# A two-layer hybrid decoder step: column halves, one order for the whole program, weights loaded twice

## The chip, the cores and the metric

The kernel runs on all 8 NeuronCores of one Trainium2 chip. Each core computes one prompt sequence and 16 sample sequences with the whole network; the cores do not talk to each other. The metric is the device time of the slowest core, in us. An execution can fall into a slow state, in which the cores of one die show a lower granted clock; only fast executions are compared here. The granted clock is the share of full speed that the profile shows for TensorE. TensorE, VectorE, ScalarE and GpSimd are PE, DVE, ACT and POOL in the profile's lines; PEld is TensorE's weight load.

## The reference, cut to what matters

```python
# per layer, prompt (2064 tokens a core) and sample (16 x 8 tokens a core) share the weights
x = x + 0.5 * swiglu(rmsnorm(x, norm_ffn1[l]), w_ffn1_gu[l], w_ffn1_down[l])   # D 1024, D_FF 2816
x = x + mixer(rmsnorm(x, norm_mix[l]), ...)                                    # RG-LRU group + gated linear attention
x = x + 0.5 * swiglu(rmsnorm(x, norm_ffn2[l]), w_ffn2_gu[l], w_ffn2_down[l])
# after two layers: rmsnorm(x, norm_final)
```

Both mixer groups carry a state along the sequence (a scan; a 64 x 128 matrix per head), so the tiles of a mixer follow each other. FFN columns are independent of each other. That difference is what the change uses.

## The kernel before

The 2192 columns lie in five tiles; each FFN and each mixer takes all of them before the next begins, with barriers around the mixer.

```python
TILES = [(0, 400), (400, 512), (912, 512), (1424, 512), (1936, 256)]
# ...
            ffn(l, 0, base, do_norm=not prenormed)
            full_barrier()
            if do_mixer:
                mixer(l, base + NJ)
                full_barrier()
            # ... ffn(l, 1, ...)
```

The root mean square of a norm is a Sqrt on ScalarE and a reciprocal on VectorE; a mixer has 5 such tiles for its norm and 20 for the head norms:

```python
P.op("act", lambda h: h.activation(out=rsa[:, :n], in_=psN[:, :n], func=AF.Sqrt, scale=1.0 / D, bias=EPS), ...)
P.op("dve", lambda h: h.reciprocal(out=rsa[:, :n], in_=rsa[:, :n]), ...)
```

An FFN chunk is 128 of the 2816 FFN columns, and the ring is the set of buffers into which the weights are loaded in turn. One slot of the ring (11 slots) holds gate, up and down columns of one chunk, 768 KB; the mixer's weights are 10 slots, loaded once per layer. Inside an FFN step or a mixer a small list scheduler orders the instructions; across them it does not look.

## Time and profile before

| | before |
|---|---|
| median | 3657 us (3654 to 3697, 5 runs) |
| TensorE busy | 2850 us, 78% |
| VectorE / ScalarE busy | 1820 us, 50% / 971 us, 27% |
| mean granted clock | 0.88 |
| HBM read | 189 MB |

The busy share of TensorE is no good measure of how near it is to its peak: the Trainium skill says so ("Perfetto Trace Analysis", "Identifying the Most-Contended Engine"), and the trace agrees that the two differ: in the first 43 us of the changed kernel TensorE is busy 15.8 us with matmuls priced at 8.0.

### The profile page before, as it was taken

What the parts mean: (1) busy time and instruction counts of PE and PEld (TensorE: products, weight loads), DVE (VectorE), ACT (ScalarE), POOL (GpSimd) and SP (SyncE); (2) the same over time, 40 slices, a digit from 0 to 9 for tenths busy, and PEclk for the clock granted to TensorE, in tenths of its full rate; (3) what the DMA queues carried; (4) which work ended last, traced back from release to release, by engine and by line L of the source; (5) the groups of instructions that cost most, each with busy time, mean ns of one, the idle gap of its engine ahead of it and who ended that gap; (6) DMA issues with size and microseconds to landing.
All of it is one profiled execution on the core that took longest, in us unless ns stands there. A gap on an engine that the chain in (4) does not pass through costs nothing.

```text
span 3655.7 us, 43632 instructions; the slowest of 8 cores (3628.5 to 3655.7 us)
## 1 busy us (share of the span) xinstructions
PE 2850.2 (78%) x14312; PEld 1389.2 (38%) x14312; DVE 1820.4 (50%) x3210; ACT 971.4 (27%) x1762; POOL 75.3 (2%) x147
## 2 busy tenths in 40 slices
PE   1899998577664379999879999956756536999994
PEld 0455553232222235554435554422223212555542
DVE  2433344666674454334543334456676546443345
ACT  2211112544552231111221111154454323111122
POOL 2000000000000000000000000000000000000000
PEclk9999999788876589999989999977878757999997
DMA  9022223000002441111111111110000135111002
GB/s 200 1 35 35 35 45 54 1 1 1 1 1 35 46 68 35 35 35 35 27 27 35 35 35 35 36 29 1 1 1 1 13 44 93 33 37 27 1 19 81
DMA packets 70715, 119.74 MB, mean 33 GB/s; under 512 B 42560, under 2 KB 47328, under 8 KB 70496
## 3 DMA queue, kind: packets, MB, share of 16 engines
q0 software_dynamic: 18320, 85.52, 13.4%
q1 hardware_dynamic: 52176, 31.42, 4.3%
q8 instruction: 122, 2.00, 0.2%
q14 instruction: 97, 0.79, 0.1%
HBM read 188.72 MB, written 13.71 MB: 55 GB/s over the span
## 4 chain that ended last, share of the span: by engine, by line
PE 66%; DVE 12%; DMA 7%; ACT 7%; issue 5%; SPq 2%; DVEq 0%; ACTq 0%
PE ps L460 18%; PE ps L433 18%; PE ps L438 18%; PE ps L650 5%; PE ps L962 3%; DMA scr<-S 2%; SPq L368 2%; PE ps L762 2%; DVE scr L412 2%; DMA cTo<-scr 2%; PE ps L396 1%; DVE scr L934 1%; ACT L708 1%; DVE scr L409 1%; ACT scr L394 1%
## 5 line engine op out<-in xcount | busy, mean ns | idle before, releaser
L438 PE MATMUL ps<-scr,ring 128*128 128x512 bf16 (+2 forms) x3520 | 850.1, 349 | 12.5 <-DVE scr L446 12.5
L433 PE MATMUL ps<-scr,ring 128*128 128x512 bf16 (+2 forms) x3520 | 855.3, 350 | 1.6 <-ACT scr L444 1.4
L460 PE MATMUL ps<-scr,ring 128*128 128x512 bf16 (+2 forms) x3520 | 707.5, 357 | 108.0 <-DVE x L464 106.4
L446 DVE TENSOR_TENSOR scr<-ps,scr 128x512 bf16<-128x512 f32 (+2 forms) x440 | 252.5, 610 | 1050.0 <-PE ps L438 868.2
L444 ACT ACTIVATE scr<-ps 128x512 f32<-128x512 f32 (+2 forms) x440 | 214.9, 533 | 1585.6 <-PE ps L433 1390.4
L464 DVE SCALAR_TENSOR_TENSOR x<-ps,x 128x512 f32<-128x512 f32 (+2 forms) x960 | 563.8, 612 | 88.7 <-PE ps L460 74.7
L460 PEld LDWEIGHTS ps<-scr,ring 128*128 128x128 bf16 x3520 | 342.0, 100 | 453.4 <-issue 175.3
L438 PEld LDWEIGHTS ps<-scr,ring 128*128 128x128 bf16 x3520 | 345.0, 98 | 326.0 <-issue 20.5
L433 PEld LDWEIGHTS ps<-scr,ring 128*128 128x128 bf16 x3520 | 342.1, 98 | 317.4 <-issue 20.8
L650 PE MATMUL ps<-scr,ring 128*128 128x512 bf16 (+4 forms) x1360 | 398.9, 433 | 73.9 <-ACT scr L662 40.5
L650 PEld LDWEIGHTS ps<-scr,ring 128*128 128x128 bf16 (+1 forms) x1360 | 148.0, 115 | 235.8 <-issue 180.0
L962 PE MATMUL ps<-scr,ring 128*128 128x512 bf16 (+2 forms) x640 | 179.8, 404 | 59.4 <-DVE scr L748 25.1
L396 PE MATMUL ps<-scr,ones 128*128 128x512 bf16 (+2 forms) x240 | 101.9, 447 | 132.9 <-ACT scr L394 109.1
L394 ACT ACTIVATE scr<-x 128x512 bf16<-128x512 f32 (+2 forms) x240 | 127.1, 562 | 256.5 <-PE ps L396 103.8
L409 DVE RECIPROCAL scr<-scr 128x512 f32<-128x512 f32 (+2 forms) x30 | 86.7, 2890 | 144.0 <-ACT scr L407 144.0
L762 PE MATMUL ps<-ring,scr 128*128 128x256 bf16 (+1 forms) x576 | 113.2, 278 | 46.7 <-DVE scr L412 45.4
L412 DVE SCALAR_TENSOR_TENSOR scr<-x,cols_sb,scr 128x512 bf16<-128x512 f32 (+2 forms) x240 | 144.5, 669 | 4.1 <-DVE scr L409 1.0
L377 POOL DMA_DIRECT2D ring<-wslots x108 | 57.2, 536 | 3287.9 <-PE ps L433 1722.7
L962 PEld LDWEIGHTS ps<-scr,ring 128*128 128x128 bf16 x640 | 66.2, 109 | 141.5 <-issue 108.4
L934 DVE RECIPROCAL scr<-scr 128x512 f32<-128x512 f32 (+2 forms) x40 | 115.5, 2887 | 7.4 <-ACT scr L932 7.4
L966 DVE TENSOR_TENSOR x<-ps,x 128x512 f32<-128x512 f32 (+2 forms) x80 | 47.9, 613 | 125.8 <-PE ps L762 69.9
L396 PEld LDWEIGHTS ps<-scr,ones 128*128 128x128 bf16 x240 | 23.9, 102 | 198.4 <-issue 190.5
(140 smaller groups left out, 1712.4 us busy)
## 6 DMA issues: line engine op xcount, KB each, us to landing
ring<-wslots POOLq DMA_DIRECT2D x108, 768.0 KB, 14.8
scr<-S SPq DMA_DIRECT2D x16, 512.0 KB, 5.4
x<-xT SPq DMA_DIRECT2D x24, 256.0 KB, 16.9
yT<-scr SPq DMA_DIRECT2D x24, 256.0 KB, 2.0
Sos<-scr SPq DMA_DIRECT2D x8, 512.0 KB, 4.7
x<-xT SPq DMA_DIRECT2D x8, 200.0 KB, 23.3
yT<-scr SPq DMA_DIRECT2D x8, 200.0 KB, 1.9
x<-xT SPq DMA_DIRECT2D x8, 128.0 KB, 8.0
```

Source lines behind the costliest of these rows:

```text
L394: P.op("act", lambda h, kc=kc, sqa=sqa: h.activation(out=sqa[:, :n], in_=x[:, kc, s:s + n], func=AF.Square), reads=[("x", kc, ti)], writes ...
L396: P.op("pe", lambda h, kc=kc, sqa=sqa: h.matmul(psN[:, :n], lhsT=ones[:], rhs=sqa[:, :n], start=(kc == 0), stop=(kc == KC - 1)), reads=[sq ...
L412: P.op("dve", lambda h, kc=kc: h.scalar_tensor_tensor(out=dst_fn(kc, s, n), in0=x[:, kc, s:s + n], scalar=cols[:, gcol + kc:gcol + kc + 1] ...
L433: P.op("pe", lambda h, kc=kc, sl=sl, gb=gb: h.matmul(psG[gb][:, :n], lhsT=ring[:, sl, kc * 128:(kc + 1) * 128], rhs=xn[:, kc, s:s + n], st ...
L438: P.op("pe", lambda h, kc=kc, sl=sl, gb=gb: h.matmul(psU[gb][:, :n], lhsT=ring[:, sl, 1024 + kc * 128:1024 + (kc + 1) * 128], rhs=xn[:, kc ...
L444: P.op("act", lambda h, gb=gb, sb=sb: h.activation(out=sg[:, sb, :n], in_=psG[gb][:, :n], func=AF.Silu), reads=[("psG", gb)], writes=[("sg ...
L446: P.op("dve", lambda h, gb=gb, sb=sb, jj=jj: h.tensor_tensor(out=hbuf[:, hb, jj, :n], in0=psU[gb][:, :n], in1=sg[:, sb, :n], op=ALU.mult), ...
L460: P.op("pe", lambda h, mc=mc, sl=sl, db=db, jj=jj: h.matmul(psD[db][:, :n], lhsT=ring[:, sl, 2048 + mc * 128:2048 + (mc + 1) * 128], rhs=h ...
L464: P.op("dve", lambda h, mc=mc, db=db: h.scalar_tensor_tensor(out=x[:, mc, s:s + n], in0=psD[db][:, :n], scalar=0.5, in1=x[:, mc, s:s + n], ...
L650: P.op("pe", lambda h, kc=kc, lhs=lhs: h.matmul(mU[ub][:m, :n], lhsT=lhs, rhs=xnt[:, kc, :n], start=(kc == 0), stop=(kc == KC - 1)), reads ...
L762: P.op("pe", lambda h, kc=kc, pr=pr, rv=rv, cs=cs, cl=cl: h.matmul(mV[:cl, pr * 256:(pr + 1) * 256], lhsT=xnt[:, kc, cs:cs + cl], rhs=rv[: ...
L962: P.op("pe", lambda h, mc=mc, ic=ic, rsl=rsl, pos=pos, ub=ub: h.matmul(mU[ub][:, :n], lhsT=ring[:, rsl, pos * 1024 + mc * 128:pos * 1024 + ...
```

## The change

Its intent: never let TensorE stand, by running the mixer of one half of the columns under the FFN of the other. It is a rewrite of nearly all lines; this is its core, abridged, with some hunks in words. Of the instructions that are ready, the scheduler takes the lowest prio first.

```diff
-TILES = [(0, 400), (400, 512), (912, 512), (1424, 512), (1936, 256)]
+TILES = [(0, 272), (272, 384), (656, 384), (1040, 384), (1424, 384), (1808, 384)]
+HALVES = [[0, 1, 2], [3, 4, 5]]
-R = 11                         # slots of gate + up + down
+NGU, NDN, NPG = 6, 5, 7        # slots: gate/up, down, mixer page
...
+        for l in range(2):
+            ffn(l, 0, 0, first=(l == 0))
+            # ... norms of half 1
+            ffn(l, 0, 1)
+            mixer(l, 0)
+            # ... norms of half 0
+            ffn(l, 1, 0)
+            mixer(l, 1)
+            # ... norms of half 1
+            ffn(l, 1, 1, after=final_norm if l == 1 else None)
+        P.run(**cfg)           # one list scheduler over all instructions; PSUM banks are given out by it
...
-    Sqrt on ACT, reciprocal on DVE
+    P.op("act", [Ln(scale, bias=EPS), Exp(scale=-0.5)], ..., tbl="L")
...
+    pick on TensorE: mixer matmuls prio 0, FFN matmuls prio 1
```

FFN weights are loaded once per half and the mixer's 28 pages once per tile. Smaller things change too: Silu replaces a Tanh form in the head gate, the GeLU takes one VectorE pass fewer, 128-partition operations replace pairs of 64-partition ones, and the small recurrent states go in and out in single transfers.

## The prediction

> **What bounds the kernel now.** I read the slices first (part 2 of the page), to see where TensorE is dense and what clock it is granted.
>
> ```profile
> PE   1899998577664379999879999956756536999994
> PEclk9999999788876589999989999977878757999997
> ```
>
> The kernel alternates: four dense stretches (the SwiGLU blocks, called FFN here) and two thin ones (the two mixers), where the clock falls too. A cut of the span into stretches, at bounds that I chose from the slices, sizes this; the columns are length, then busy us (instructions) of each engine, granted clock, DMA share, GB/s.
>
> ```profile
> 0.00:78.00 78.00, 6.88 (x14) 1.46 (x14) 12.88 (x34) 11.68 (x22) 24.05 (x50) 1.00 0.99 191
> ...
> 183.00:598.00 415.00, 410.67 (x2202) 212.09 (x2200) 170.45 (x297) 44.65 (x92) 10.07 (x19) 1.00 0.23 37
> 598.00:1279.00 681.00, 396.36 (x1801) 173.49 (x1800) 411.98 (x790) 298.69 (x531) 5.28 (x10) 0.74 0.12 16
> ...
> 1371.00:1736.00 365.00, 362.46 (x1937) 187.32 (x1936) 145.67 (x249) 38.81 (x80) 8.44 (x16) 1.00 0.19 35
> ...
> 2376.00:3040.00 664.00, 382.11 (x1752) 167.74 (x1752) 404.06 (x770) 294.65 (x523) 3.70 (x7) 0.74 0.10 16
> ```
>
> In dense FFN the matmuls come one per 188 ns (365 us / 1937) at full clock: nothing is left there but the matmuls. The mixers take 681 + 664 = 1345 us with no engine above 61% busy: they are chains of latencies, fenced off by a barrier on both sides, with no FFN matmuls to fill the holes. The rest is 78 us of start (DMA 0.99) and 722 us of mixed stretches, norms before an FFN and the final norms. In the chain that ended last, taken in order of time, one accumulation group of the last FFN product gives the bare rate of TensorE:
>
> ```profile
> 2026.17 6.91 PE ps L460 x32
> ```
>
> 32 matmuls of 512 columns in 6.91 us is 216 ns each. The costliest groups, and the finer list by shape (last three lines), give the unit prices:
>
> ```profile
> L464 DVE SCALAR_TENSOR_TENSOR x<-ps,x 128x512 f32<-128x512 f32 (+2 forms) x960 | 563.8, 612 | 88.7 <-PE ps L460 74.7
> L409 DVE RECIPROCAL scr<-scr 128x512 f32<-128x512 f32 (+2 forms) x30 | 86.7, 2890 | 144.0 <-ACT scr L407 144.0
> L934 DVE RECIPROCAL scr<-scr 128x512 f32<-128x512 f32 (+2 forms) x40 | 115.5, 2887 | 7.4 <-ACT scr L932 7.4
> ...
> L464 DVE SCALAR_TENSOR_TENSOR x<-ps,x 128x400 f32<-128x400 f32 x192 | 103.2, 571 | 16.5 <-PE ps L460 9.4
> L464 DVE SCALAR_TENSOR_TENSOR x<-ps,x 128x256 f32<-128x256 f32 x192 | 75.2, 420 | 7.2 <-PE ps L460 5.5
> L444 ACT ACTIVATE scr<-ps 128x400 f32<-128x400 f32 x88 | 40.9, 501 | 327.4 <-PE ps L433 226.5 <-PE ps L438 82.8 <-DVE scr L446 18.1
> ```
>
> **What the Trainium skill says.** (1) "TensorE: Matmul & The Clock Gate", section "Wait — 56ns, not 53.3ns?": a warm matmul of N columns is issued every N/2.4 + about 2.5 ns, 215.7 at 512. The 216 above agrees; I price TensorE with it. (2) The same page, Part 1: an idle window of about 3.4 us halves the clock, and once three cores of a die run dense matmuls the clock is held at 13/16. The first fits the mean 0.74 of the mixers; the second does not show: eight cores run, and the dense stretches have 1.00. The measurement decides. (3) "ScalarE: Activation LUTs", "What ACT_TABLE_LOAD costs" and "Table sets": a switch of table costs 1283 ns plus a drain of about 1380; Ln and Exp share a set. The trace has the 1283 but no drain:
>
> ```profile
> 631.46 1.28 ACT L775 ACT_TABLE_LOAD   x1
> 632.75 0.59 ACT L775 ACTIVATE scr<-ps,sm 128x400 f32<-128x400 f32 x1
> ```
>
> The function starts 1.29 us after the load. (4) "DMA: Bandwidth & Descriptors", "Where 436 GB/s comes from": about 358 GB/s of HBM per core when both cores of a pair stream. The weight queue here wrote 85.52 MB (bf16, read as f32) in 13.4% of 3655.7 us of its engines: 175 GB/s written, 349 read. It agrees.
>
> **The change part by part.** It is a rewrite. The 2192 columns go in two halves of three tiles (272, then five of 384); one list scheduler orders all instructions of the whole program; there is no barrier. The mixer of one half can run while the FFN of the other half fills TensorE: FFN1 half 0 alone, then FFN1 half 1 with mixer half 0, then FFN2 half 0 with mixer half 1, then FFN2 half 1 beside the next layer's FFN1 half 0, and so on.
>
> *TensorE, the floor.* One chunk over all tiles is 5 x 162.5 + 115.8 = 928 ns. FFN: 4 x 22 x 24 = 2112 chunks, 1961 us. Sums of squares: seven norms x 8 = 56 chunks, 52 us. Mixer per layer: 16 projections, 8 output columns and the low-rank one, 25 x 8 = 200 chunks, 186 us; gates and small sums 14 chunks, 13; v, 144 matmuls of 512, 31; attention and states, some 450 matmuls of 128 or less at 56 ns, 25: 255 us, 510 for two. Sum 2523 us.
>
> *VectorE.* From the rows of 400 and 256 columns I interpolate to 384 and 272: 554 and 437 ns plain, 613 and 496 where a column scalar is read. FFN accumulation 192 x 3.21 = 616 us; silu product 88 x 3.21 = 282; norms 56 x 3.56 = 199; a mixer tile about 42 us (four recurrent chunks of 5.6, two head pairs of 7.7, output 4.4), 530 us for both layers with the sample states. Total about 1630 against 1820: the reciprocals (202 us in the two rows) are gone, replaced by Ln and Exp(-0.5) on ScalarE.
>
> *ScalarE.* Silu 88 x (5 x 0.488 + 0.394) = 249 us; squares 169; Ln/Exp of the norms 42; a mixer tile about 48 us, 575 in all. Table switches: 11 Ln/Exp batches in each of 12 mixer tiles and 30 norms are 162 batches among Silu and Tanh; two switches each, if none merge, is 324; I take 280 x 1.28 = 359. Total about 1400 us against 971.
>
> *DMA.* FFN weights are loaded twice (277 MB read) and 28 mixer pages for every tile (336 x 0.524 = 176 MB): 453 MB instead of 170. Written: 226 MB / 175 GB/s = 1290 us of the 16 engines, under half of the span, and all hidden if the rings of 6, 5 and 7 slots run far enough ahead. GpSimd issues 688 loads at 0.54 us, 370 us.
>
> *Start and end.* TensorE now begins after one tile of x and two weight slots; 8.7 MB of first loads at the 191 GB/s of the first stretch is 45 us, partly used: I charge 40 where it was 78 and more. The end is one tile's norm, about 12.
>
> *Sum.* Four stretches carry mixer and FFN together: FFN half 245, mixer half 128, norms 7 = 380 us of TensorE each. Beside it ScalarE has about 285 us (31 silu, 160 mixer, 15 norms, 80 switches) and VectorE 275. I choose 91% for TensorE there: 417 us, so 37 x 4 = 150 us of holes. The four FFN halves outside lose 2%, 20 us. 2523 + 40 + 12 + 150 + 20 = 2745 us. The gain of 912 us comes mainly from the 1345 us of mixers, which shrink to 510 us of matmuls plus holes, and from norms hidden inside other work.
>
> **The rivals.** *The mixer's chain becomes the bound.* A mixer tile has 127 us if it is to hide (380/3). Before, the mixer needed about 150 us for a tile of 512 alone on all engines. In the new one a head pair is some 19 hops of about 24 us of work, roughly 40 us with waits; the two pairs go one after the other, because PSUM banks of this class are given out in program order and the transposed keys have one buffer. With v, norm and output I reach 105 us. For this rival: ScalarE at 75% and VectorE at 72% in the stretch lengthen each hop. If a tile takes 160 us, each stretch is 480 us: 2523 + 72 + 4 x 100 = 2995. *ScalarE becomes the bound* through table switches (Silu must answer each FFN chunk within microseconds): at 500 switches it gains 280 us of work, and TensorE falls to perhaps 80% in the stretches, 475 us: about 2975. *The weights come late.* In such a stretch 34.6 + 44 MB are read, 39 MB written, 225 us at 175 GB/s of 417: enough on average, but one in-order GpSimd queue waits for three rings. Five per cent lost there would be 83 us more, about 2830. *The clock.* Dense, all engines busy, a limiter at 13/16 would make 2523 into 3105, so about 3300; 1.00 in the dense stretches speaks against it. *Nearly perfect overlap*, with the next layer's FFN as extra filler, gives 2600.
>
> **Range and chances.** The floor with start and end is 2575, and nothing can undercut it; I take 2615 as the low end. The high end is a mixture of the first two rivals at half strength, 2910. Reaching 3584 (2% faster) needs 1000 us of holes, far more than any of these gives. Faster 0.96, same 0.02, slower 0.02.
>
> **What would show it.** Right: TensorE at 9 in nearly all slices and clock 9; dense FFN matmuls of 384 columns one per 163 ns; no RECIPROCAL rows; VectorE near 1630 us, ScalarE near 1400; HBM read near 470 MB; a dense last FFN half, 245 us. Wrong: slices of 6 to 8 in the four mixed stretches with matmuls waiting for ScalarE (table rival), for mixer groups (chain rival) or weight landings (DMA rival); clock 8 in dense slices. A time over 2910 means that the mixed stretches were not bound by TensorE; one under 2615 that the static order held almost without holes.

## The result, and the profile after

The changed kernel takes 2669.24 us (2666.45 to 2992.88, 9 runs, of which two were slow) against 3659.38 (17 runs, seven of them plainly slow). The medians of the fast runs alone are 2667 and 3657, a gain of 990 us. The ratio of the fast runs is 0.7299, 95% interval 0.7291 to 0.7307: 27% less time. A ratio here is the mean time of one kernel's fast runs over that of the other's of the same rounds, so it is not quite the ratio of the medians. The time lies inside the range, 76 us under the predicted 2745.

The slices of the changed kernel, to be held against the two lines of before:

```profile
PE   5799999999999999999999999999999999999998
PEclk9899999999999999999999999999999999999999
```

The alternation is gone: TensorE is at 9 from the third slice to the last but one, and the clock in all slices but the second. The totals per engine:

```profile
PE 2588.5 (97%) x16740; PEld 1584.3 (59%) x16752; DVE 1497.3 (56%) x3115; ACT 1283.3 (48%) x2446; POOL 368.9 (14%) x699
```

The stretches, at bounds that I set where the loss changes; columns as in the prediction (length; PE, PEld, DVE, ACT and POOL; granted clock, DMA share, GB/s):

```profile
0.00:43.00 43.00, 15.84 (x63) 7.52 (x64) 12.79 (x44) 17.73 (x37) 5.64 (x14) 0.90 0.84 174
43.00:84.00 41.00, 41.00 (x276) 27.02 (x275) 18.86 (x39) 17.66 (x31) 8.42 (x16) 0.98 0.91 170
84.00:111.00 27.00, 8.06 (x31) 2.84 (x29) 3.20 (x6) 7.14 (x16) 2.16 (x5) 0.65 0.98 204
111.00:266.00 155.00, 154.95 (x1033) 102.17 (x1034) 65.00 (x132) 21.53 (x45) 14.33 (x27) 0.98 0.43 71
266.00:1132.00 866.00, 856.31 (x5595) 519.05 (x5600) 541.54 (x1144) 539.24 (x1025) 142.65 (x269) 1.00 0.64 101
1132.00:1598.00 466.00, 465.82 (x3022) 295.09 (x3020) 225.30 (x448) 101.16 (x196) 45.12 (x85) 1.00 0.43 74
1598.00:2464.00 866.00, 858.13 (x5582) 518.46 (x5588) 529.40 (x1112) 538.68 (x1021) 138.41 (x261) 1.00 0.61 103
2464.00:2597.00 133.00, 133.00 (x821) 80.06 (x819) 58.09 (x109) 16.73 (x34) 11.68 (x22) 1.00 0.42 74
2597.00:2665.00 68.00, 55.35 (x330) 32.11 (x328) 43.15 (x84) 23.47 (x43) 0.54 (x1) 0.91 0.22 74
```

I counted the matmuls of each stretch by their columns in the list by shape, priced them at N/2.4 + 2.5 ns, and took the rest of the stretch as lost:

| stretch | what runs | matmuls priced, us | lost, us |
|---|---|---|---|
| 0 to 43 | first loads | 8.0 | 35.0 |
| 43 to 84 | first FFN units | 40.6 | 0.4 |
| 84 to 111 | sums of squares, few FFN matmuls | 5.0 | 22.0 |
| 111 to 266 | FFN alone | 152.6 | 2.4 |
| 266 to 1132 | mixers and FFN, layer 0 | 826.3 | 39.7 |
| 1132 to 1598 | FFN | 465.6 | 0.4 |
| 1598 to 2464 | mixers and FFN, layer 1 | 828.3 | 37.7 |
| 2464 to 2597 | FFN alone | 133.4 | none |
| 2597 to 2665 | last unit, final norm | 53.6 | 14.4 |

The priced matmuls sum to 2514 us of 2665. In the mixed stretches TensorE issues at 95.4% of its rate (826.3 / 866), where the two mixers of before held it busy 58% of the time at a clock of 0.74. The 151 us lost lie half in the mixed stretches and half outside them, nearly all of that at the two ends. So most of the old time went away because the FFN's matmuls moved into time in which the mixer only waits. That is a claim about cause, and the experiments test it.

### The profile page after: what moved, and what is told of

It is laid out like the page before. It is cut to its first block, busy times and chain, and to the rows that moved or that the text cites. A ratio compares the mean times of both kernels' runs of the same rounds, so it can differ in the third digit from the quotient of the medians.

```text
span 2664.9 us, 46662 instructions; the slowest of 8 cores (2658.3 to 2664.9 us)
## 1 busy us (share of the span) xinstructions
PE 2588.5 (97%) x16740; PEld 1584.3 (59%) x16752; DVE 1497.3 (56%) x3115; ACT 1283.3 (48%) x2446; POOL 368.9 (14%) x699
## 3 DMA queue, kind: packets, MB, share of 16 engines
q0 software_dynamic: 99856, 227.48, 53.5%
## 4 chain that ended last, share of the span: by engine, by line
PE 89%; DVE 5%; DMA 3%; SPq 1%; issue 1%; ACT 1%; DVEq 0%; ACTq 0%
PE ps L399 87%; DMA x<-xT 2%; PE ps L398 2%; DVE x L386 2%; SPq L406 1%; DVE xn L386 1%; DVE xnt L386 1%; DVE hb L392 0%; DMA S0f<-S 0%; DMA yT<-xnt 0%; DMA Sos<-S0f 0%; DVE S0f L386 0%; DVE Fb L740 0%; DVE Fb L386 0%; PE ps L856 0%
## 5 line engine op out<-in xcount | busy, mean ns | idle before, releaser
L399 PE MATMUL ps<-xn,rgu 128*128 128x384 bf16 (+1 forms) x8448 | 1386.5, 320 | 2.5 <-DVE xn L386 2.1
L399 PEld LDWEIGHTS ps<-xn,rgu 128*128 128x128 bf16 x8448 | 825.5, 98 | 487.1 <-issue 11.3
L386 DVE SCALAR_TENSOR_TENSOR x<-ps,x 128x384 f32<-128x384 f32 (+1 forms) x1152 | 588.9, 535 | 361.4 <-PE ps L399 336.0
L399 PE MATMUL ps<-hb,rdn 128*128 128x384 bf16 (+1 forms) x4224 | 710.7, 318 | 9.3 <-DVE x L386 6.5
L380 ACT ACTIVATE sg<-ps 128x384 f32<-128x384 f32 (+1 forms) x528 | 248.4, 475 | 929.9 <-PE ps L399 661.6
L399 PEld LDWEIGHTS ps<-hb,rdn 128*128 128x128 bf16 x4224 | 407.1, 98 | 255.4 <-issue 22.7
L392 DVE TENSOR_TENSOR hb<-ps,sg 128x384 bf16<-128x384 f32 (+1 forms) x528 | 275.0, 535 | 380.8 <-PE ps L399 337.0
L436 POOL DMA_DIRECT2D rpg<-wmx x336 | 178.4, 535 | 800.4 <-PE ps L399 760.0
L399 PE MATMUL ps<-xnt,rpg 128*128 128x384 bf16 (+1 forms) x1536 | 265.6, 318 | 0.8 <-DVE xnt L386 0.7
L399 PEld LDWEIGHTS ps<-xnt,rpg 128*128 128x128 bf16 x1536 | 148.1, 98 | 89.8 <-issue 2.9
L380 ACT ACT_TABLE_LOAD x124 | 159.1, 1283 | 10.8 <-PE ps L399 7.5
```

What stands on the lines that cost most here:

```text
L380: P.op("act", lambda h: h.activation(out=o_(), in_=i_(), func=func, scale=scale, **kw), reads, writes, dur=ac(n, ptr + 1), tbl=tbl, prio=prio)
L386: P.op("dve", lambda h: h.scalar_tensor_tensor(out=o_(), in0=a_(), scalar=scalar, in1=b_(), op0=op0, op1=op1), reads, writes, dur=dv(n), p ...
L392: P.op("dve", lambda h: h.tensor_tensor(out=o_(), in0=a_(), in1=b_(), op=op), reads, writes, dur=dv(n), prio=prio)
L399: return lambda h: h.matmul(o_(), lhsT=lhsT, rhs=rhs, start=start, stop=stop)
L436: P.op("pool", lambda h: h.dma_start(out=rpg[:, s, :], in_=wmx_d[l, k]), reads=["gate"] if pg_n[0] <= NPG else [], writes=[("pg", s)], dur ...
```

## The experiments

The *filler theory*: the gain is FFN matmuls in the holes of the mixer. The *cheaper-work rival*: the gain is the work that is gone (reciprocals, a leaner mixer, norms hidden, tile shapes), and the overlap adds little. Both parts are in the change, so each is undone alone.

### The overlap undone

```diff
+            P.stage += 1       # the scheduler lets PE, ACT and DVE start nothing of a stage
             mixer(l, 0)        # before everything of the stage ahead is done; loads stay free
+            P.stage += 1       # the same around mixer(l, 1)
```

> The changed kernel with its order alone altered: PE, ACT and DVE finish all FFN work of a stage before a mixer half starts, and the mixer before the next FFN; loads stay free to run ahead. Filler theory (the gain is FFN matmuls in the holes of the mixer): a mixer tile alone takes about 105 us, 12 of them 1260, FFN and norms about 2020, start and end 70: 3250 to 3450 us, clock near 0.75 in the mixer stretches. Cheaper-work rival (the gain comes from the reciprocals that are gone, the cheaper mixer formulas, the tile shapes and the hidden norms, so the overlap is worth little): under 2850 us.

It took 3318 us (median of the fast runs, 3315 to 3325), 0.908 of the kernel before (0.9055 to 0.9104). Its slices:

```profile
PE   6799999556999666599999999975669986657998
PEclk9899999677999777799999999987779997778999
```

The valleys are back, four now, one for each mixer half. The stretches of two of its mixer halves, in the columns as above:

```profile
560.00:850.00 290.00, 173.87 (x910) 91.41 (x912) 128.46 (x275) 191.75 (x378) 45.94 (x87) 0.76 0.52 80
1090.00:1410.00 320.00, 189.31 (x1022) 94.42 (x1022) 151.96 (x321) 198.62 (x390) 47.52 (x90) 0.75 0.49 86
```

By the first and last projection matmul, cut to 10 us, the four halves took 290, 320, 280 and 310 us: 1200 us, or 100 us for each of 12 tiles, where no engine is busy above two thirds. In the changed kernel the same matmuls are spread over about 830 us per layer, longer than the 610 of the two halves alone, and hidden. The filler theory is confirmed and the rival falls as a main cause: of the 990 us gained, some 650 (3318 - 2667) go with the overlap alone, what starts and ends at the fences included. The other 340 are the rival's share: the mixers themselves are about 145 us shorter than the 1345 of before (whose bounds were chosen from slices, so that this is rough), and some 195 come from the start, the norms beside the FFN and the barriers; I did not part these further.

### FFN first

```diff
-  ... [G], dur=8 * mmd(n), prio=1)      # the same for up and down products
+  ... [G], dur=8 * mmd(n), prio=-1)     # mixer matmuls keep prio 0
```

> The changed kernel with FFN matmuls ahead of mixer matmuls in the scheduler's choice for TensorE, nothing else. Theory (the mixer tiles are one long chain that must run first, FFN is only filler): the filler is used up before the mixer, which then runs bare, 3000 to 3400 us. Rival (TensorE is kept full whatever goes first, because work is plentiful): within 2% of the changed kernel, 2640 to 2720 us.

One fast execution: 3305 us. Nothing of the work or of the freedom to overlap is changed, yet it is as slow as the fence, and its slices look the same:

```profile
PE   6799999567799668499999989985869986776997
```

Filler has to be kept for the time in which the chain waits. The rival, that there is always enough work, allowed 2720 us at most and is wrong by 585.

### Reciprocals put back into the changed kernel

```diff
-  [Ln, Exp(scale=-0.5)] on ACT
+  Sqrt on ACT;  h.reciprocal(out=dst, in_=dst) on DVE      # 42 norm tiles, 48 head norms
```

> The changed kernel with Sqrt on ACT and RECIPROCAL on DVE put back in place of Ln and Exp at all 42 norms and 48 head norms: some 90 x 2.5 us = 225 us more on DVE. Filler theory: DVE has 44% idle and TensorE is the bound, so it costs 1 to 3%, 2695 to 2750 us. Cheaper-work rival: the removed reciprocals are a main part of the gain, and at least 150 us come back, 2820 us or more.

2732 us (2731 to 2735), ratio to before 0.7476: 2.4% over the changed kernel (0.7476 / 0.7299). The new rows on VectorE:

```profile
L946 DVE RECIPROCAL Fb<-Fb 128x384 f32<-128x384 f32 (+1 forms) x48 | 115.5, 2421 | 16.9 <-ACT Fb L942 16.9
L455 DVE RECIPROCAL rsf<-rsf 128x384 f32<-128x384 f32 (+1 forms) x30 | 73.0, 2433 | 51.8 <-ACT rsf L453 51.8
L455 DVE RECIPROCAL Fb<-Fb 128x384 f32<-128x384 f32 (+1 forms) x12 | 29.1, 2425 | 0.9 <-ACT Fb L453 0.9
```

They sum to 218 us; VectorE's total rose by 197, from 1497 to 1694, and the time by 64. So about two thirds of it are hidden even at 62% VectorE. The 64 us are those of the whole swap: the table loads on ScalarE rose too, from 247 to 276.

### Ln and Exp put into the kernel before, and the reciprocal made cheap

```diff
-  Sqrt; h.reciprocal(out=rsa, in_=rsa)
+  Ln; Exp(scale=-0.5)                                           # first run
+  Sqrt; h.tensor_scalar(out=rsa, in0=rsa, scalar1=-0.35, scalar2=1.4, op0=mult, op1=add)   # second, wrong on purpose
```

> The kernel before with all its reciprocals replaced by Ln and Exp, as the changed kernel has it, and nothing else. Filler theory: 75 reciprocals of 2.9 us lie in chains of latencies, about half of them on the path that ends last, and Ln and Exp of 0.6 us each take their place: 40 to 120 us less, 3540 to 3620 us. Cheaper-work rival (this is a main part of the 990 us gained): 3450 us or less. If the DVE time was beside the path: 3640 to 3670.

This missed every number of mine: 3678 to 3687 us in its fast runs, 0.8% slower than before (ratio 1.0077, 1.0061 to 1.0094), although VectorE's busy time fell from 1820 to 1612 us. Its table loads in the rows of the head norms and of the first gate, and those of the kernel before below:

```profile
L932 ACT ACT_TABLE_LOAD x40 | 51.3, 1283 | 0.7
L696 ACT ACT_TABLE_LOAD x26 | 33.4, 1283 | 3.2 <-PE ps L847 2.2
```

```profile
L932 ACT ACT_TABLE_LOAD x4 | 5.1, 1283 | 0.1
L696 ACT ACT_TABLE_LOAD x18 | 23.1, 1283 | 4.4 <-PE ps L847 3.5
```

Before, 36 of 40 head norms found their Sqrt table already loaded; with Ln every one needs a load. Over all rows the loads rose from 150 to 211, 78 us of ScalarE. That is a candidate; the other is that the reciprocals lay beside the path all along. The second run tells them apart.

> The kernel before with each reciprocal replaced by one multiply-add on the same tile (a wrong result on purpose): about 190 us less of VectorE, no table load added or removed. If the reciprocals lie on the path that ends last: 60 to 150 us less, 3510 to 3600 us, and then the table switches of Ln and Exp ate that gain in the earlier run. If they lie beside it: 3640 to 3670 us, and then the Ln and Exp run lost its 28 us to the switches alone.

3521 to 3528 us in its fast runs, against 3654, the only fast run of the kernel before in the same rounds: about 130 us less. VectorE's total:

```profile
PE 2819.7 (80%) x14312; PEld 1382.6 (39%) x14312; DVE 1636.2 (46%) x3210; ACT 968.6 (27%) x1762; POOL 75.3 (2%) x147
```

It fell by 184 us, and 130 of them were on the path. So in the old order the reciprocals did cost, and Ln and Exp cost more: the swap as a whole loses 28 us there, some 160 worse than the multiply-add. ScalarE's total explains 121 of it as work (1089 us with Ln and Exp, 969 with the multiply-add): 78 for the loads, the rest for the Exps. How much of that work and of the waiting behind it lies on the path is not shown. In the changed kernel, whose scheduler has a price for a switch and gathers the batches, the same swap gains 64.

### Twice the Silu

```diff
-  act(sg, G, AF.Silu)
+  P.op("act", [silu, silu], ...)         # 528 more instructions, same result
```

> The changed kernel with every Silu of the FFN done twice (same input, same output, the second after the first): 528 more ACT instructions of 0.47 us, 250 us more of ACT, about 58% of the span. Theory (TensorE is the bound, ScalarE has room): at most 1.5% more, 2669 to 2705 us. Rival of the prediction (ScalarE is near the bound in the mixed stretches): 4% or more, 2775 us up.

Its two undisturbed runs took 2674.0 and 2674.5 us, some 6 us (0.2%) over the changed kernel. The totals:

```profile
PE 2592.3 (97%) x16752; PEld 1586.5 (59%) x16752; DVE 1498.4 (56%) x3115; ACT 1530.9 (57%) x2978; POOL 367.6 (14%) x699
```

248 us more of ScalarE cost 6. The table rival of the prediction falls: ScalarE is far from being the bound.

### Fewer weight slots

```diff
-NGU, NDN, NPG = 6, 5, 7
+NGU, NDN, NPG = 4, 4, 5
```

> The changed kernel with fewer weight slots: gate and up 6 to 4, down 5 to 4, mixer pages 7 to 5; same bytes. Theory (transfers are hidden because the rings run ahead, not because bandwidth is plentiful: with 4 slots for groups of 4 nothing is ahead): TensorE waits at the group changes, 2700 to 2800 us. Rival (DMA at half load hides anyhow): 2660 to 2690 us.

2736 to 2739 us in the fast runs, ratio 0.7488, 2.6% over the changed kernel, with the same bytes. The theory's range was right, but not its picture of TensorE waiting at the group changes: the scheduler ordered anew for the smaller rings, only 6 us of TensorE's waits end by name with a landing of weights, and the holes are spread over the mixed stretches (70 and 67 us lost, counted as above over that run's own mixed stretches, instead of 40 and 38). So the deeper rings are worth some 70 us; through what the shallower ones lose them is not shown, and most of the transfers stay hidden with them too.

### No margin in the scheduler

```diff
-_CFG = {}
+_CFG = {"slack": 0.0}       # was 450 ns before a matmul that waits for another engine
```

> The changed kernel with the scheduler's margin, 450 ns added before a matmul that waits for another engine, set to 0. Theory (the fixed order holds the holes down because it asks for results with room to spare): TensorE's queue is held up by late ACT and DVE results in the mixed stretches, 2690 to 2760 us. Rival (the plenty of FFN filler does it, the margin is worth little): 2655 to 2685 us.

2665 to 2667 us in the fast runs: no difference to the changed kernel's 2667 that two sets of rounds could show. The theory is wrong and the rival right: the margin is worth nothing, the filler is what fills.

### The hole at 84 us, and the first 43

```diff
 act(sqf, x, AF.Square, ...  reads [("x", kc, ti)]
+                             + ["gate2"]    # written by the seventh unit of the first FFN half; tiles 3 to 5, layer 0
```

> The changed kernel with one more dependency: the squares of the norms of tiles 3 to 5 in the very first FFN wait for the seventh unit of the first half, so their sums no longer stand in TensorE's queue before FFN matmuls that are ready. Theory (the 22 us lost at 84 to 111 us are TensorE's in-order queue held up by sums whose x has not landed): 2642 to 2654 us. Rival (the weight and x transfers themselves limit TensorE there, so the hole only moves): 2663 to 2672 us.

2646.27 us (2644.04 to 2648.80, 4 runs), ratio 0.7239 (0.7225 to 0.7253). Against the changed kernel that is 0.7239 / 0.7299 = 0.992, and it is the fastest version here. The same stretch:

```profile
84.00:111.00 27.00, 23.79 (x148) 15.01 (x147) 4.45 (x9) 3.75 (x8) 3.18 (x6) 0.94 1.03 210
```

148 matmuls instead of 31. So TensorE's queue was the cause: sums of squares of tiles 3 to 5 stood in front, their x had not landed, and FFN matmuls that were ready stood behind. The order is the scheduler's, whose model must have had x land earlier than it did.

The same cure for tile 2, in the first 43 us:

> The changed kernel with the delayed norms of tiles 3 to 5 of the run before, and the norm of tile 2 held back too, to the first unit of the first FFN half. Theory (35 us are lost before 43 us, part of it because sums of tiles 1 and 2 stand ahead of matmuls of tile 0 that are ready): 4 to 10 us under the 2646 of that run, 2636 to 2642. Rival (the first 43 us are bound by the transfers of x and the first weights): 2643 to 2649 us.

Four runs at 2645 to 2649 us and one at 2670, ratio 0.7256 (0.7226 to 0.7286): no gain over the run above, inside the rival's range. But the edit didn't do what it was meant to. TensorE's queue in this run (idle time before an instruction in brackets):

```profile
32.98 0.74 PE L399 MATMUL ps<-sqf,ones 128*128 128x384 bf16 x2 [2.26 <-ACT sqf L380]
34.01 0.74 PE L399 MATMUL ps<-sqf,ones 128*128 128x384 bf16 x2 [0.29 <-ACT sqf L380]
37.67 0.89 PE L399 MATMUL ps<-sqf,ones 128*128 128x384 bf16 x2 [2.93 <-ACT sqf L380]
38.36 2.02 PE L399 MATMUL ps<-xn,rgu 128*128 128x272 bf16 x8
```

The sums of tile 2 still stand before the third chunk of tile 0 (the last line), whose weights had landed at 27.4 us. Some 6 us of TensorE's idle time there are queue order once more. That the landing of x and of the first weights bounds the rest of the first 43 us fits the DMA share of 0.84, but this run doesn't show it.

## Why the prediction was right, point by point

- *TensorE is the bound, floor 2523 us.* Counted 2514 us. Right. In the stretch of 384 columns alone (2464 to 2597) a matmul comes every 162 ns (133 us / 821), predicted 163.
- *Overlap is where the gain comes from.* Right: some 650 of 990 us by the fence. A tile of the mixer alone, estimated at 105 us, took 100.
- *Holes in the mixed stretches 150 us, beside them 20.* This is the term that was mis-sized most: 77 and 3. The 91% was chosen, not derived; measured it is 95.4%. The prediction feared long waits with ScalarE at 75% and VectorE at 72% of the stretch's matmul time; measured they are 65% and 64 to 66% of it, doubling Silu costs 6 us, and leaving out the margin costs nothing. The order keeps filler at hand: the two mixed stretches of a layer hold 826 us of matmuls, not the 760 predicted, and the sign of a dense last FFN half of 245 us did not come, because only 187 us of priced matmuls were left after 2464 us.
- *Start 40 us.* 57 us: 35 before 43 us, mostly transfers as far as is known, and 22 through the queue order shown above, which the prediction did not see. *End 12*: 14.
- These terms make up the difference: 2514 + 57 + 14 + 77 + 3 = 2665 us, the profiled span, instead of 2745. The start was charged too little and the holes too much, so the errors partly cancel.
- *VectorE 1630 us.* 1497 busy. The prediction summed durations, while the profile's busy time counts once what overlaps: over all rows of the changed kernel, count times mean duration is 1640 us. So the prices fit in sum, and were held against the wrong figure. In the same way the row of the FFN accumulation has 1152 x 535 ns = 616 us of durations, as predicted, and 589 busy. *ScalarE 1400.* 1283 busy, 1368 as a sum of durations, with 247 table loads for the 280 assumed. Doubling Silu shows that ScalarE does not set the time.
- *DMA 1290 us of the engines, hidden.* The weight queue took 53.5% of 2665, 1426 us, nearly all hidden; smaller rings cost some 70 us. HBM read 468 MB, predicted near 470. GpSimd 369 us, predicted 370.
- *The clock rival*: mean granted clock 0.989 or more on every core in the fast state. It did not come.
- *Two slips in the working, without effect on the sum.* ScalarE's 285 us a stretch count 160 for a mixer half, where three tiles of 48 us make 144. The high end of 2910 is called both first rivals at half strength; half of each together would be 2745 + 125 + 115 = 2985.

## What to carry to other kernels

Where one stage is a chain of latencies and another is dense matmul, let the chain go first and keep the dense work as filler; the same instructions ordered the other way round gave back 638 of the 990 us gained here (one run). A replacement that costs less by itself can lose through a table switch, so price it in the order in which it will run. And look for what stands at the head of TensorE's queue at the start: one added dependency was worth 21 us.

## What the Trainium skill lacked or had wrong

- "TensorE: Matmul & The Clock Gate", Part 1, puts the clock of a die at 13/16 whenever three of its cores run dense matmuls. In the fast runs here all eight cores run matmuls for 97% of the span at a mean granted clock of 0.989 and above. A lower clock came only in some executions: in the slowest of the changed kernel (2993 us) one die had 0.865 to 0.872 and 2978 to 2991 us, the other 0.99 and 2659 to 2667. In the changed kernel and its variants the lowest mean of a whole die was 0.806 (3222 us, a slow run with fewer slots), near the page's 13/16. The page does not tell of executions of one kernel that differ in this way.
- "ScalarE: Activation LUTs", "What ACT_TABLE_LOAD costs", adds a drain of about 1380 ns to the load of 1283 ns. The load is 1283 ns in every row; in the lines that the prediction shows, the function after it began 1.29 us after the load's start, with no drain between, and the load 0.02 us after the end of the instruction before it.
- "DMA: Bandwidth & Descriptors" prices loads by their size; I found no figure there for loads that cast f32 to bf16. In the kernel before, the weight queue wrote 175 GB/s (read twice that) with packets of 4.67 KB on average (85.52 MB, 18320 packets); in the changed kernel it wrote 227.48 MB in 53.5% of 2664.9 us, 160 GB/s, with packets of 2.28 KB (99856 packets).
